# FFN up-projection of a diffusion trunk: seven block products per pair of output tiles

## Chip, cores and metric

The program runs on one core of a Trainium2 chip, in one launch. The metric is the device time of an execution in microseconds; the time of a kernel is the median of several executions. The engines are named as in the profile: PE is TensorE (matrix products), DVE VectorE, ACT ScalarE, POOL GpSimd, SP SyncE, which issues the transfers. A line number such as L101 is a line of the kernel's file.

## The reference

One inference step of a trunk of two layers on 512 latent and 128 context tokens of width 1024, in float32. Each layer has three mixers and then a gated MLP (FFN), which the change concerns. Cut to the FFN:

```python
def dwconv3(x, w, b):
    T = x.shape[1]
    xp = jnp.pad(x, ((0, 0), (1, 1), (0, 0)))
    return xp[:, :T] * w[0] + xp[:, 1:T + 1] * w[1] + xp[:, 2:] * w[2] + b
...
    u = dwconv3(h @ P['w_up'][l], P['ffn_conv_w'][l], P['ffn_conv_b'][l])
    x = x + g2 * ((jax.nn.silu(u[..., :D_FF]) * u[..., D_FF:]) @ P['w_down'][l])
```

Here h is the normed and modulated input (1024 features), D_FF is 2816, and w_up has 2 x 2816 columns: the first half is gated by SiLU and multiplied with the second. Latent and context tokens take the same weights; the convolution runs within each of the two groups.

## The kernel before

Tensors lie feature-major: a tile holds 128 features on the partitions and all 640 tokens (512 latent, 128 context) in its columns. The tokens are worked in two halves of 320 columns, one PSUM bank each. Every float32 product is made of two float32r parts: a value is cast to its high part `hi`, and `lo` is the value less `hi`; a product is hi·x_hi + hi·x_lo + lo·x_hi. So an output tile of the up-projection takes 8 feature tiles x 3 terms x 2 halves = 48 matmuls of 320 columns.

`weights` (L90) loads a chunk of weights (128 x 1024, 512 KB) into one of three slots "raw", and splits it 512 columns at a time: the cast on ACT (L100), the subtraction (L101) on POOL and DVE in turns (`alt`). The high and low parts have four slots each, "whi" and "wlo". `mm` (L117) issues the matmuls of an output tile, and `split` (L104) does the same split for an activation (L110 cast, L111 subtraction).

`ffn` (L908) works on 22 pairs of hidden tiles, a gate tile and a value tile each. `up(f)` makes the two products of pair f; `conv` follows each: ACT reads the product from PSUM and writes bias + w1·u to SBUF (L163), and four DVE operations add the left and the right neighbour (L165, L167), each for the 512 latent and for the 128 context columns, with the shifted operand read from PSUM. `glu` applies SiLU on ACT (L915), multiplies gate and value on POOL (L916), and splits the result for the down-projection. After a part of the pairs (FFN_PARTS, three parts of 7, 7 and 8) the down-projection adds that part to the residual x, in 8 output tiles.

The FFN's first pair is made within `handoff` (L449): the residual product before the FFN, the norm that follows it, and the first two up-products overlap, one half of the tokens after the other. The normed tiles are written there by DVE (L371 scales by the inverse root, L356 makes the low part) and ACT. `mod_step` makes the modulation vectors of what comes next: 2 MB of w_mod are loaded (L259) into eight slots "mw" of 256 KB and go through PE (L264). In the FFN it runs after pairs 2 and 4 and after every second down tile, while anything is left to do (7 vectors of 512 columns in layer 0, 2 in layer 1).

A scheduler orders the instructions of all engines when the program is built; only the matmuls that are pinned keep the order in which they were written. Each engine and each queue then works through its own list in order.

Of the kernel before, what the change touches and what calls it, by code (L numbers as in the profile page):

```python
# [16 lines left out]
P = 128  # L17
D = 1024
KD = D // P
NS = 512  # L20
# [36 lines left out]
class Tags:  # L57
    """A pool with a number of slots for each tag."""
# [8 lines left out]
class Trunk:  # L67
# [17 lines left out]
    def alt(self):  # L85
        """VectorE and GpSimd in turns, for work that either can do."""
# [3 lines left out]
    def weights(self, src, n):  # L90
        """Loads a chunk and splits it exactly into two float32r parts, 512 columns at a time."""
# [25 lines left out]
    def mm(self, acc, w, k0, xs, halves=(0, 1), ks=None, pin=False):  # L117
        """acc[m, t] = sum_k w[k, m] x[k, t]; w holds the tiles k0.. of len(xs)."""
# [41 lines left out]

    def conv(self, dst, acc, w0, w1, w2, bias):
# [8 lines left out]
    # ---------------------------------------------------------------- set-up  # L170
    def consts(self):
# [8 lines left out]
        # silu of the two conditionings, padded to 32 columns  # L180
# [23 lines left out]
    def layer_consts(self, l):  # L204
        nc, I = self.nc, self.I
        lp = self.lp
# [9 lines left out]
        # tensors of the mixers  # L216
        self.sgw = self.t(lp, [P, H, P], F32, "lc", 4)
        nc.sync.dma_start(self.sgw, I["sg_wT"][l])
        self.sgb = self.t(lp, [P, H, P], F32, "lc", 4)
# [688 lines left out]
    def ffn(self, l, h, accs, x, p2, nxt):  # L908
# [27 lines left out]
        for f0, f1 in FFN_PARTS:  # L936
            # the next part's first tile fills the time in which this part's last one is finished
            for f in range(len(acts), min(f1 + 1, NF)):
                up(f)
                if f in (2, 4):  # L940
                    self.mod_step((p2, "mw", 1))
# [200 lines left out]
```

## Time and profile before

| | |
|---|---|
| time, median of three runs | 2443.1 us (2442.36 to 2447.7) |
| span of the profiled execution | 2439.1 us |
| around the span, by the median | 4.0 us |
| PE busy | 2408.0 us, 99% |
| DVE busy | 1134.0 us, 46% |
| ACT busy | 944.8 us, 39% |
| POOL busy | 669.9 us, 27% |
| largest group of matmuls (L129, h by the high parts) | 6464 matmuls, 1246.9 us |

The span is the profiled execution from its first to its last instruction; the time of a run also holds what lies around it. Busy time counts an engine's own instructions, so two engines that are both busy may be in each other's way without the table showing it; that is to be read from the timelines.

### The profile page before, as it was taken

How to read it: one execution, taken by the hardware profiler on the slowest of the kernel's cores; microseconds unless marked ns; L12 is line 12 of the kernel's file. 1: busy time of each engine (PE TensorE's matmuls, PEld its weight loads, DVE VectorE, ACT ScalarE, POOL GpSimd, SP SyncE). 2: the span in 40 equal slices, each digit the busy share in tenths (PEclk: the TensorE clock that was granted, in tenths of full speed). 3: DMA queues.
4: the chain of work that ended last, by engine and by line, in shares of the span. 5: the costliest groups of instructions: out<-in, count | busy, mean ns of one | idle time of the engine just before them, and what ended most of it. 6: DMA issues, size and time to landing. Idle time of an engine off the chain costs nothing.

```text
span 2439.1 us, 40662 instructions
## 1 busy us (share of the span) xinstructions
PE 2408.0 (99%) x16708; PEld 2313.9 (95%) x16708; DVE 1134.0 (46%) x2111; ACT 944.8 (39%) x1728; POOL 669.9 (27%) x486
## 2 busy tenths in 40 slices
PE   8999999999999999999999999999999999999998
PEld 7999999999598999999999999999986989999998
DVE  5455545553146433424446455455532454244344
ACT  4433335544145322323454332455442543232334
POOL 2322232332222322313213222323322223232231
PEclk9999999999999999999999999999999999999999
DMA  8221221123544234222322212211233432222222
GB/s 282 74 73 64 65 78 62 60 72 132 173 147 160 69 109 140 72 75 79 103 80 70 74 64 66 76 54 62 97 114 120 147 96 74 79 74 73 81 72 69
DMA packets 88761, 227.39 MB, mean 93 GB/s; under 512 B 9472, under 2 KB 23936, under 8 KB 88576
## 3 DMA queue, kind: packets, MB, share of 16 engines
q1 hardware_dynamic: 88576, 224.80, 28.2%
q8 instruction: 131, 2.15, 0.4%
q14 instruction: 54, 0.44, 0.1%
HBM read 217.41 MB, written 7.35 MB: 92 GB/s over the span
## 4 chain that ended last, share of the span: by engine, by line
PE 96%; DVE 3%; ACT 1%; DMA 0%; issue 0%; SPq 0%; DVEq 0%; POOL 0%; POOLq 0%; ACTq 0%
PE acc L129 77%; PE acc L156 6%; PE ms L264 3%; PE ms L869 2%; PE ms L840 2%; PE ms L156 1%; PE ms L862 1%; PE ms L716 1%; PE ms L718 1%; PE ms L705 1%; DVE x L439 0%; PE ms L670 0%; PE ms L536 0%; PE ms L277 0%; PE ms L327 0%
## 5 line engine op out<-in xcount | busy, mean ns | idle before, releaser
L129 PE MATMUL acc<-h,whi 128*128 128x320 f32 x6464 | 1246.9, 311 | 5.0 <-DVE h L356 3.3
L129 PEld LDWEIGHTS acc<-h,whi 128*128 128x128 f32 x6464 | 1019.3, 188 | 32.1 <-issue 19.3
L100 ACT CAST whi<-raw 128x512 fp32r<-128x512 f32 x596 | 365.3, 614 | 1038.1 <-PE acc L129 787.9
L101 POOL TENSOR_TENSOR wlo<-raw,whi 128x512 fp32r<-128x512 f32 (+1 forms) x298 | 390.7, 1311 | 1355.1 <-ACT whi L100 1304.7
L129 PE MATMUL acc<-h,wlo 128*128 128x320 f32 x3232 | 755.4, 310 | 0.0
L129 PEld LDWEIGHTS acc<-h,wlo 128*128 128x128 f32 x3232 | 544.2, 188 | 3.5 <-issue 3.4
L101 DVE TENSOR_TENSOR wlo<-raw,whi 128x512 fp32r<-128x512 f32 (+1 forms) x298 | 241.2, 810 | 451.0 <-ACT whi L100 435.0
L129 PE MATMUL acc<-act,whi 128*128 128x320 f32 x1408 | 269.6, 310 | 0.0
L129 PEld LDWEIGHTS acc<-act,whi 128*128 128x128 f32 x1408 | 222.0, 188 | 4.2 <-issue 2.5
L129 PE MATMUL acc<-act,wlo 128*128 128x320 f32 x704 | 165.5, 309 | 0.0
L129 PE MATMUL acc<-y,whi 128*128 128x320 f32 x768 | 154.3, 314 | 1.7 <-DVE y L114 1.7
L499 DVE SCALAR_TENSOR_TENSOR x<-acc,mod,x 128x128 f32<-128x128 f32 (+3 forms) x136 | 66.3, 527 | 181.3 <-PE acc L129 181.3
L165 DVE SCALAR_TENSOR_TENSOR cw<-acc,vec,cw 128x511 f32<-128x511 f32 (+1 forms) x176 | 95.7, 544 | 115.1 <-ACT cw L163 114.0
L156 PE MATMUL acc<-whi,h 128*128 128x256 f32 x768 | 145.7, 283 | 0.0
L129 PEld LDWEIGHTS acc<-y,whi 128*128 128x128 f32 x768 | 121.2, 188 | 17.3 <-issue 11.7
L156 PEld LDWEIGHTS acc<-whi,h 128*128 128x128 f32 x768 | 123.0, 192 | 0.0
L129 PEld LDWEIGHTS acc<-act,wlo 128*128 128x128 f32 x704 | 119.1, 188 | 0.0
L916 POOL TENSOR_TENSOR cw<-cw,cw 128x640 f32<-128x640 f32 x44 | 69.2, 1573 | 156.5 <-DVE cw L167 151.9
L156 PE MATMUL acc<-wlo,h 128*128 128x256 f32 x384 | 108.7, 283 | 0.0
L167 DVE SCALAR_TENSOR_TENSOR cw<-acc,vec,cw 128x511 f32<-128x511 f32 (+1 forms) x176 | 96.7, 550 | 6.0
L129 PE MATMUL acc<-y,wlo 128*128 128x320 f32 x384 | 92.1, 315 | 0.0
L848 ACT ACTIVATE wk<-ms,mx 128x640 f32<-128x640 f32 (+1 forms) x80 | 56.7, 709 | 76.6 <-DVE mx L846 73.2
(257 smaller groups left out, 2425.0 us busy)
## 6 DMA issues: line engine op xcount, KB each, us to landing
raw<-w_in_f SPq DMA_DIRECT2D x98, 512.0 KB, 3.4
raw<-w_up SPq DMA_DIRECT2D x88, 512.0 KB, 3.3
wk<-w_mod SPq DMA_DIRECT2D x72, 256.0 KB, 3.4
mw<-w_mod SPq DMA_DIRECT2D x72, 256.0 KB, 5.7
raw<-w_down SPq DMA_DIRECT2D x32, 448.0 KB, 3.3
raw<-w_in_v SPq DMA_DIRECT2D x24, 512.0 KB, 3.7
raw<-w_branch SPq DMA_DIRECT2D x24, 512.0 KB, 3.3
mw<-w_mod SPq DMA_DIRECT2D x16, 512.0 KB, 8.8
```

The lines of the kernel that those rows point to most:

```text
L100: nc.scalar.copy(hi, raw[:, a:b])
L101: self.alt().tensor_sub(lo, raw[:, a:b], hi.bitcast(F32))
L129: ins = nc.tensor.matmul(acc[:, s], a[:, sl], b[:, s], start=k == 0 and i == 0, stop=k == last and i == 2)
L156: nc.tensor.matmul(accs[b], a[:, bs], w[:, sl], start=first and b % 2 == 0, stop=last and (b % 2 == 1 or b == NB - 1))
L165: nc.vector.scalar_tensor_tensor(dst[:, a + 1 : b], acc[:, a : b - 1], w0, dst[:, a + 1 : b], ALU.mult, ALU.add)
L167: nc.vector.scalar_tensor_tensor(dst[:, a : b - 1], acc[:, a + 1 : b], w2, dst[:, a : b - 1], ALU.mult, ALU.add)
L264: ins = nc.tensor.matmul(ps[j : j + 32, 0:width], self.cs[:, k, :], raws[k], start=k < 4, stop=k >= 4, tile_position=(0, j))
L499: self.nc.vector.scalar_tensor_tensor(x[:, a:b], acc[:, a:b], g[:, k, i : i + 1], x[:, a:b], ALU.mult, ALU.add)
L840: nc.tensor.matmul(ps[:, s : s + 320], st[:, qs], kk[:, s : s + 320], start=i == 0, stop=i == 1)
L848: nc.scalar.activation(e[:, 0:nk], ps[:, 0:nk], AF.Exp, bias=mx, scale=scale, accum_out=sm[:, j : j + 1])
L869: nc.tensor.matmul(po, at[:, c * P : (c + 1) * P], vv, start=c == 0, stop=c == n - 1)
L916: nc.gpsimd.tensor_mul(cs[0], cs[0], cs[1])
```

## The change

Pairs 2 to 21 of each layer, 20 of 22, are made by seven block products. The weights of a pair form a 2 x 2 block matrix: gate and value tile (rows), first and second four feature tiles (columns); the input h forms another: first and second four feature tiles (rows), first and second half of the tokens (columns). The eight block products of before become seven products of sums of blocks (`quarter`, 4 feature tiles x 3 terms = 12 matmuls of 320 columns each): 84 matmuls a pair in place of 96. The sums of weight blocks s1, s2, s3 are made on DVE and POOL and split again into high and low parts (`halves`: ACT cast, low part on the given engine). The sums of input blocks are made once per layer (`token_factors`), from the tiles `u` before the norm's shift is added; 16 additions on POOL, and subtractions, casts and low parts on DVE and ACT. Products that several outputs share stay in PSUM and are added to there; ACT and DVE copy and add the partial sums into two SBUF tiles, from which `conv` now reads. A pair's last two products (`seven_back`), its convolution and its `glu` come after the first two products of the next pair (`flush`).

Other edits: four parts of 5, 6, 5 and 6 pairs; `mod_step` in the FFN loads through the slots "raw" of the weights, four loads of 512 KB instead of eight of 256 KB; fewer slots for activations (14 instead of 20), more for convolution tiles (10 instead of 8), 24 new ones "tx" and three "ws"; layer constants lie in another pool.

The diff's core (in `up7` and `flush` `b` are the input factors):

```diff
-FFN_PARTS = ((0, 7), (7, 14), (14, 22))
+FFN_PARTS = ((0, 5), (5, 11), (11, 16), (16, 22))
...
+    def quarter(self, acc, w, xs, first, last):
+        nc = self.nc
+        hi, lo = w
+        for k, (xh, xl) in enumerate(xs):
+            sl = slice(k * P, (k + 1) * P)
+            for i, (a, b) in enumerate(((hi, xh), (hi, xl), (lo, xh))):
+                ins = nc.tensor.matmul(acc, a[:, sl], b, start=first and k == 0 and i == 0, stop=k == 3 and i == 2,
+                                       skip_group_check=not first)
+                self.tc.keep_in_program_order(ins)
+
+    def halves(self, src, eng):
+        hi = self.t(self.wp, [P, 512], F32R, "whi")
+        lo = self.t(self.wp, [P, 512], F32R, "wlo")
+        self.nc.scalar.copy(hi, src)
+        eng.tensor_sub(lo, src, hi.bitcast(F32))
+        return hi, lo
+
+    def seven_open(self, p, srcs):
+        nc = self.nc
+        r0, r1 = (self.t(self.wp, [P, 1024], F32, "raw") for _ in srcs)
+        for r, src in zip((r0, r1), srcs):
+            nc.sync.dma_start(r, src)
+        st = {"p": p, "r": ((r0[:, 0:512], r0[:, 512:]), (r1[:, 0:512], r1[:, 512:]))}
+        st["xy"] = self.t(self.ps, [P, 1024], F32, "acc", 2)
+        st["x"], st["y"] = st["xy"][:, 0:NHALF], st["xy"][:, 512 : 512 + NHALF]
+        st["c"] = [self.t(p, [P, NT], F32, "cw") for _ in range(2)]
+        return st
+
+    def seven_front(self, st, b):
+        nc, p = self.nc, st["p"]
+        (a11, a12), (a21, a22) = st["r"]
+        w1 = self.halves(a11, nc.vector)
+        w2 = self.halves(a12, nc.gpsimd)
+        s1, s2, s3 = (self.t(p, [P, 512], F32, "ws") for _ in range(3))
+        nc.vector.tensor_add(s1, a21, a22)
+        nc.gpsimd.tensor_add(s2, s1, a11)
+        nc.vector.tensor_add(s3, a11, a21)
+        st["s"] = s1, s2, s3
+        self.quarter(st["x"], w1, b["11"], True, False)
+        nc.scalar.copy(st["c"][0][:, 0:NHALF], st["x"])
+        self.quarter(st["y"], w2, b["21"], True, True)
+        nc.vector.tensor_add(st["c"][0][:, 0:NHALF], st["y"], st["c"][0][:, 0:NHALF])
+
+    def seven_mid(self, st, b):
...
+        w6 = self.halves(s2, nc.gpsimd)
+        w5 = self.halves(s1, nc.vector)
+        w7 = self.halves(s3, nc.gpsimd)
+        nc.gpsimd.tensor_add(s2, s2, a12)
+        self.quarter(x, w6, b["t2"], False, False)
+        nc.scalar.copy(c0[:, NHALF:NT], x)
+        self.quarter(z, w5, b["t1"], True, False)
+        self.quarter(x, w7, b["t3"], False, False)
+        nc.scalar.copy(c1[:, NHALF:NT], x)
+        nc.vector.scalar_tensor_tensor(c1[:, NHALF:NT], z, -1.0, c1[:, NHALF:NT], ALU.mult, ALU.subtract)
+
+    def seven_back(self, st, b):
...
+        w4 = self.halves(st["r"][1][1], nc.vector)
+        w3 = self.halves(st["s"][1], nc.gpsimd)
+        self.quarter(st["x"], w4, b["t4"], False, True)
+        nc.scalar.mul(c1[:, 0:NHALF], st["x"], -1.0)
+        self.quarter(st["z"], w3, b["22"], False, True)
+        nc.vector.tensor_add(c0[:, NHALF:NT], st["z"], c0[:, NHALF:NT])
+        return c0, c1
+
+    def token_factors(self, p, h, u, sh):
...
+        for k in range(4):
+            for kk in (k, k + 4):
+                for c, d, g in ((0, NS, 0), (NS, NT, 1)):
+                    nc.gpsimd.tensor_scalar_add(u[kk][:, c:d], u[kk][:, c:d], sh[:, kk, g : g + 1])
+            u0, u1 = u[k], u[k + 4]
+            f = self.t(p, [P, 2, NHALF], F32, "cw")
+            nc.vector.tensor_sub(f[:, 0], u0[:, half[0]], u0[:, half[1]])
+            nc.vector.scalar_tensor_tensor(f[:, 1], f[:, 0], -1.0, u1[:, half[1]], ALU.mult, ALU.subtract)
+            for j, n in enumerate(("t1", "t2")):
+                hi, lo = (self.t(p, [P, NHALF], F32R, "tx") for _ in range(2))
+                nc.scalar.copy(hi, f[:, j])
+                nc.vector.tensor_sub(lo, f[:, j], hi.bitcast(F32))
+                b[n].append((hi, lo))
...
+        def flush():
+            for f, st in pending:
+                glu([conv(2 * f + i, c) for i, c in enumerate(self.seven_back(st, b))])
+            pending.clear()
+
+        def up7(f):
+            st = self.seven_open(p2, [self.I["w_up"][l, i] for i in (2 * f, 2 * f + 1)])
+            self.seven_front(st, b)
+            flush()
+            self.seven_mid(st, b)
+            pending.append((f, st))
...
-                    self.mod_step((p2, "mw", 1))
+                    self.mod_step((self.wp, "raw", 2))
```

How the instructions now stand. First POOL, in the pairs of layer 0's second part. The names: raw, whi and wlo are weights and their parts, ws a sum of weight blocks, cw a convolution tile, act an activation's part. Before, two pairs of output tiles:

```order
L916 TENSOR_TENSOR cw_1315_8212<-cw_1315_8212,cw_1322_8277 128x640
L101 TENSOR_TENSOR wlo_1356_8466<-raw_1352_8459,whi_1355_8465 128x512
L101 TENSOR_TENSOR wlo_1363_8531<-raw_1359_8524,whi_1362_8530 128x512
L916 TENSOR_TENSOR cw_1331_8348<-cw_1331_8348,cw_1338_8413 128x640
L101 TENSOR_TENSOR wlo_1370_8598<-raw_1368_8595,whi_1369_8597 128x512
L111 TENSOR_TENSOR act_1340_8422<-cw_1331_8348,act_1339_8421 128x640
L101 TENSOR_TENSOR wlo_1377_8663<-raw_1375_8660,whi_1376_8662 128x512
```
And after, one pair (L202 makes s2, L220 adds a12 to it, L177 makes low parts, L1035 is the gated product):

```order
L202 TENSOR_TENSOR ws_1615_9752<-ws_1614_9751,raw_1605_9736 128x512
L177 TENSOR_TENSOR wlo_1613_9748<-raw_1605_9736,whi_1612_9747 128x512
L177 TENSOR_TENSOR wlo_1620_9788<-ws_1588_9600,whi_1619_9787 128x512
L1035 TENSOR_TENSOR cw_1594_9665<-cw_1594_9665,cw_1595_9671 128x640
L177 TENSOR_TENSOR wlo_1627_9837<-ws_1615_9752,whi_1626_9836 128x512
L111 TENSOR_TENSOR act_1597_9680<-cw_1594_9665,act_1596_9679 128x640
L220 TENSOR_TENSOR ws_1615_9752<-ws_1615_9752,raw_1605_9736 128x512
L177 TENSOR_TENSOR wlo_1631_9845<-ws_1616_9753,whi_1630_9844 128x512
```
Where POOL had two low parts of weights, a gated product and every other time a low part of an activation in a pair, it has four low parts and two sums beside the same two.

Second DVE, in the same pairs: before, one tile's convolution out of PSUM (acc) between low parts:

```order
L101 TENSOR_TENSOR wlo_1540_9852<-raw_1538_9849,whi_1539_9851 128x512
L111 TENSOR_TENSOR act_1520_9709<-cw_1511_9635,act_1519_9708 128x640
L165 SCALAR_TENSOR_TENSOR cw_1527_9771<-acc_1521_9712,vec0_7_90,cw_1527_9771 128x511
L167 SCALAR_TENSOR_TENSOR cw_1527_9771<-acc_1521_9712,vec0_7_90,cw_1527_9771 128x511
L165 SCALAR_TENSOR_TENSOR cw_1527_9771<-acc_1521_9712,vec0_7_90,cw_1527_9771 128x127
L167 SCALAR_TENSOR_TENSOR cw_1527_9771<-acc_1521_9712,vec0_7_90,cw_1527_9771 128x127
L101 TENSOR_TENSOR wlo_1547_9917<-raw_1545_9914,whi_1546_9916 128x512
```
And after, from the convolution of a pair to the last partial sum of the next one (L284 and L286 are the convolution, L177 low parts, L203 s3, L208 and L226 partial sums out of PSUM, acc and ms):

```order
L284 SCALAR_TENSOR_TENSOR cw_1594_9665<-cw_1554_9437,vec0_7_90,cw_1594_9665 128x511
L284 SCALAR_TENSOR_TENSOR cw_1594_9665<-cw_1554_9437,vec0_7_90,cw_1594_9665 128x127
L284 SCALAR_TENSOR_TENSOR cw_1595_9671<-cw_1555_9438,vec0_7_90,cw_1595_9671 128x511
L284 SCALAR_TENSOR_TENSOR cw_1595_9671<-cw_1555_9438,vec0_7_90,cw_1595_9671 128x127
L286 SCALAR_TENSOR_TENSOR cw_1594_9665<-cw_1554_9437,vec0_7_90,cw_1594_9665 128x511
L286 SCALAR_TENSOR_TENSOR cw_1594_9665<-cw_1554_9437,vec0_7_90,cw_1594_9665 128x127
L286 SCALAR_TENSOR_TENSOR cw_1595_9671<-cw_1555_9438,vec0_7_90,cw_1595_9671 128x511
L177 TENSOR_TENSOR wlo_1618_9784<-raw_1579_9585,whi_1617_9783 128x512
L286 SCALAR_TENSOR_TENSOR cw_1595_9671<-cw_1555_9438,vec0_7_90,cw_1595_9671 128x127
L226 SCALAR_TENSOR_TENSOR cw_1582_9590<-ms_1598_9683,cw_1582_9590 128x320
L203 TENSOR_TENSOR ws_1616_9753<-raw_1605_9736,raw_1606_9737 128x512
L208 TENSOR_TENSOR cw_1608_9741<-acc_1607_9740,cw_1608_9741 128x320
```
The convolution's shifted operand is now a cw tile in SBUF, both tiles' rows come in one piece, and low parts and partial sums stand between and behind them.

Third SP's queue, at the first pairs of layer 0's FFN. Before:

```order
L94 DMA raw_1290_8049<-w_up 128x1024
L259 DMA mw_1434_9120<-w_mod 128x512
L259 DMA mw_1435_9122<-w_mod 128x512
L94 DMA raw_1310_8154<-w_up 128x1024
L259 DMA mw_1436_9124<-w_mod 128x512
L259 DMA mw_1437_9126<-w_mod 128x512
L259 DMA mw_1438_9128<-w_mod 128x512
L259 DMA mw_1439_9130<-w_mod 128x512
L259 DMA mw_1440_9132<-w_mod 128x512
L94 DMA raw_1317_8219<-w_up 128x1024
```
And after:

```order
L94 DMA raw_1302_7997<-w_up 128x1024
L188 DMA raw_1310_8075<-w_up 128x1024
L188 DMA raw_1311_8076<-w_up 128x1024
L378 DMA raw_1330_8176<-w_mod 128x1024
L378 DMA raw_1331_8178<-w_mod 128x1024
L378 DMA raw_1332_8180<-w_mod 128x1024
L378 DMA raw_1333_8182<-w_mod 128x1024
L188 DMA raw_1336_8201<-w_up 128x1024
L188 DMA raw_1337_8202<-w_up 128x1024
L188 DMA raw_1363_8353<-w_up 128x1024
```
The loads of w_mod went to slots mw between those of the weights; now four of them take slots raw in the weights' own turn, and the loads of the next pair stand behind them.

## Rows read from the trace of the kernel before

**Rows 1.** Page, busy time by engine, and granted clock in 40 slices.
```profile
PE 2408.0 (99%) x16708; PEld 2313.9 (95%) x16708; DVE 1134.0 (46%) x2111; ACT 944.8 (39%) x1728; POOL 669.9 (27%) x486
...
PEclk9999999999999999999999999999999999999999
```

**Rows 2.** Page, chain that ended last: share of the span by engine.
```profile
PE 96%; DVE 3%; ACT 1%; DMA 0%; issue 0%; SPq 0%; DVEq 0%; POOL 0%; POOLq 0%; ACTq 0%
```

**Rows 3.** Windows: start:end, length, busy us (instructions) by engine, clock, DMA share, GB/s.
```profile
1060.00:1160.00 100.00, 100.00 (x684) 100.00 (x683) 41.27 (x66) 33.51 (x51) 28.84 (x22) 1.00 0.24 79
```

**Rows 4.** Timeline of ACT: start, duration, what; idle before in brackets.
```profile
771.32 0.88 ACT L163 ACTIVATE cw<-acc,vec 128x640 f32<-128x640 f32 x1
...
815.89 0.88 ACT L163 ACTIVATE cw<-acc,vec 128x640 f32<-128x640 f32 x1
...
822.93 0.88 ACT L163 ACTIVATE cw<-acc,vec 128x640 f32<-128x640 f32 x1
```

**Rows 5.** Timeline of PE in the norm that precedes the FFN.
```profile
742.43 0.31 PE L129 MATMUL acc<-h,wlo 128*128 128x320 f32 x1
...
742.87 0.31 PE L129 MATMUL acc<-h,wlo 128*128 128x320 f32 x1
```

**Rows 6.** Timeline of POOL, 800 to 823 us.
```profile
801.98 1.30 POOL L101 TENSOR_TENSOR wlo<-raw,whi 128x512 fp32r<-128x512 f32 x1 [5.74 <-ACT whi L100]
...
807.84 1.57 POOL L111 TENSOR_TENSOR act<-cw,act 128x640 fp32r<-128x640 f32 x1
...
819.13 1.58 POOL L916 TENSOR_TENSOR cw<-cw,cw 128x640 f32<-128x640 f32 x1 [5.29 <-DVE cw L167]
```

**Rows 7.** Timeline of DVE, 800 to 823 us.
```profile
802.72 0.75 DVE L165 SCALAR_TENSOR_TENSOR cw<-acc,vec,cw 128x511 f32<-128x511 f32 x1 [3.57 <-ACT cw L163]
...
809.03 0.93 DVE L101 TENSOR_TENSOR wlo<-raw,whi 128x512 fp32r<-128x512 f32 x1 [4.13 <-ACT whi L100]
...
811.32 0.34 DVE L165 SCALAR_TENSOR_TENSOR cw<-acc,vec,cw 128x127 f32<-128x127 f32 x1
...
816.07 0.69 DVE L101 TENSOR_TENSOR wlo<-raw,whi 128x512 fp32r<-128x512 f32 x1 [4.02 <-ACT whi L100]
...
819.58 1.67 DVE L101 TENSOR_TENSOR wlo<-raw,whi 128x512 fp32r<-128x512 f32 x1 [0.60 <-ACT whi L100]
```

**Rows 8.** Timeline of DVE, 348.5 to 351.5 us.
```profile
348.92 0.69 DVE L788 TENSOR_TENSOR qk<-qk,lc 128x512 f32<-128x512 f32 x1
```

**Rows 9.** Timeline of POOL, 348.5 to 351.5 us.
```profile
348.96 1.81 POOL L787 TENSOR_TENSOR wk<-wk,lc 128x512 f32<-128x512 f32 x1 [3.62 <-DVE wk L786]
```

**Rows 10.** Timelines of POOL and DVE, 144 to 147 us.
```profile
144.56 1.30 POOL L101 TENSOR_TENSOR wlo<-raw,whi 128x512 fp32r<-128x512 f32 x1 [5.74 <-ACT whi L100]
145.16 1.39 DVE L572 SCALAR_TENSOR_TENSOR qk<-wk,qk 128x640 f32<-128x640 f32 x1 [1.24 <-ACT wk L571]
```

**Rows 11.** Groups by shape, DVE and ACT: count, busy us, mean ns, idle before.
```profile
L309 DVE TENSOR_TENSOR sqa<-sqa,sq 128x320 f32<-128x320 f32 x56 | 27.4, 489 | 15.1 <-ACT sq L304 15.1
...
L100 ACT CAST whi<-raw 128x512 fp32r<-128x512 f32 x564 | 348.9, 620 | 983.3 <-PE acc L129 733.1 <-issue 179.0 <-PE ms L156 61.1
...
L915 ACT ACTIVATE cw<-cw 128x640 f32<-128x640 f32 x44 | 32.3, 735 | 0.0
L110 ACT CAST act<-cw 128x640 fp32r<-128x640 f32 x44 | 32.0, 728 | 52.3 <-POOL cw L916 52.3
```

**Rows 12.** Timeline of DVE at the end of the norm.
```profile
761.63 1.27 DVE L356 SCALAR_TENSOR_TENSOR h<-cw,mod,h 128x192 fp32r<-128x192 f32 x4
```

**Rows 13.** One line, L915: its table loads, ns min/median/max.
```profile
L915 ACT ACT_TABLE_LOAD  x2: 1283/1283/1283, 772.2 to 1975.2; - x2
```

**Rows 14.** Page, DMA issues: count, KB each, median us to landing.
```profile
raw<-w_up SPq DMA_DIRECT2D x88, 512.0 KB, 3.3
```

**Rows 15.** Tile mw: what its readers waited for, us and times.
```profile
  DMA mw<-w_mod: 4.7, 7
```

**Rows 16.** Windows near the start of the span.
```profile
8.00:20.00 12.00, 8.07 (x59) 7.54 (x61) 5.14 (x7) 6.37 (x11) 0.00 (x0) 0.86 1.05 390
```

More of the change, by code (lines that the diff above doesn't have):

```diff
@@ new lines, in seven_mid @@
+    def seven_mid(self, st, b):
+        nc, p = self.nc, st["p"]
+        (a11, a12), (a21, a22) = st["r"]
+        s1, s2, s3 = st["s"]
+        c0, c1 = st["c"]
+        x = st["x"]
+        z = st["z"] = self.psM()[:, 0:NHALF]
+        w6 = self.halves(s2, nc.gpsimd)
[8 more added lines that the diff above has]
+        nc.vector.scalar_tensor_tensor(c1[:, NHALF:NT], z, -1.0, c1[:, NHALF:NT], ALU.mult, ALU.subtract)
@@ new lines, in seven_back, with finish @@
+    def seven_back(self, st, b):
+        nc = self.nc
+        c0, c1 = st["c"]
+        w4 = self.halves(st["r"][1][1], nc.vector)
[6 more added lines that the diff above has]
+    def token_factors(self, p, h, u, sh):
+        nc = self.nc
+        half = (slice(0, NHALF), slice(NHALF, NT))
+        b = {n: [] for n in ("11", "21", "22", "t1", "t2", "t3", "t4")}
+        for k in range(4):
+            for n, kk, t in (("11", k, 0), ("21", k + 4, 0), ("22", k + 4, 1)):
+                b[n].append(tuple(x[:, half[t]] for x in h[kk]))
+        todo = []
+        for k in range(4):
+            for kk in (k, k + 4):
[10 more added lines that the diff above has]
+                b[n].append((hi, lo))
+            nc.vector.tensor_sub(u0[:, half[0]], u1[:, half[1]], u0[:, half[1]])
+            nc.vector.scalar_tensor_tensor(u1[:, half[0]], f[:, 1], -1.0, u1[:, half[0]], ALU.mult, ALU.subtract)
+            hi, lo = (self.t(p, [P, NHALF], F32R, "tx") for _ in range(2))
+            nc.scalar.copy(hi, u1[:, half[0]])
+            nc.vector.tensor_sub(lo, u1[:, half[0]], hi.bitcast(F32))
+            b["t4"].append((hi, lo))
+            todo.append((k, u0))
+        def finish():
+            for k, u0 in todo:
+                hi, lo = (x[:, half[1]] for x in h[k])
+                nc.scalar.copy(hi, u0[:, half[0]])
+                nc.vector.tensor_sub(lo, u0[:, half[0]], hi.bitcast(F32))
+                b["t3"].append((hi, lo))
+        return b, finish
@@ L205, in layer_consts @@
         nc, I = self.nc, self.I
-        lp = self.lp
+        lp, p1 = self.lp, self.p1
         self.vec = self.vecs[l]
@@ L222, in layer_consts @@
         for i in range(2):
-            self.rope.append(self.t(lp, [P, NS], F32, "lc", 4))
+            self.rope.append(self.t(p1, [P, NS], F32, "lc"))
             nc.sync.dma_start(self.rope[i], I["rope"][:, i, :])
-        self.ck = self.t(lp, [P, H, P], F32, "lc", 4)
+        self.ck = self.t(p1, [P, H, P], F32, "lc")
         nc.sync.dma_start(self.ck, I["cache_kT"][l])
-        self.cv = self.t(lp, [P, H, P], F32, "lc", 4)
+        self.cv = self.t(p1, [P, H, P], F32, "lc")
         nc.sync.dma_start(self.cv, I["cache_v"][l])
-        self.cn = self.t(lp, [P, 8, 129], F32, "cn", 1)
+        self.cn = self.t(p1, [P, 8, 129], F32, "cn")
         nc.sync.dma_start(self.cn, I["state"][l])
@@ L905, in branch, with ffn @@
         return out
-    def ffn(self, l, h, accs, x, p2, nxt):
+    def ffn(self, l, h, u, accs, x, p2, nxt):
         nc = self.nc
@@ L932, in up @@
             glu(cs)
+        pending = []
+        def flush():
[8 more added lines that the diff above has]
+            pending.append((f, st))
+        b, finish = self.token_factors(p2, h, u, self.mods[l, 3])
         glu([conv(i, acc) for i, acc in enumerate(accs)])
+        up(1)
+        finish()
+        done = 2
         st = self.norm_open(l + 1, 0 if nxt else None, p2, "cw")
         for f0, f1 in FFN_PARTS:
-            for f in range(len(acts), min(f1 + 1, NF)):
-                up(f)
+            for f in range(done, min(f1 + 1, NF)):
+                up7(f)
                 if f in (2, 4):
-                    self.mod_step((p2, "mw", 1))
+                    self.mod_step((self.wp, "raw", 2))
+                done = f + 1
+            end = f1 == NF
+            if end:
+                flush()
             g2 = self.mods[l, 5]
             down = lambda m: self.I["w_down"][l, m, :, f0 * P : f1 * P]
-            end = f1 == NF
             for m in range(KD - 2 if end else KD):
@@ L948, in ffn @@
                 self.mm(acc, w, 0, acts[f0:f1])
+                if m == 0:
+                    flush()
                 self.residual(x[m], acc, g2, m)
@@ L953, in ffn @@
                 elif m % 2:
-                    self.mod_step((p2, "mw", 1))
+                    self.mod_step((self.wp, "raw", 2))
         return self.handoff([down(m) for m in (KD - 2, KD - 1)], acts[f0:f1], x, g2, st,
```

13 lines of the change are left out of this document (7 added, 6 removed).

## The prediction

> **What bounds the kernel now.** I read the page's busy times and its clock row first, and the reader sees one engine: PE is busy in 99% of the span and its granted clock is at the full level throughout [rows 1]. The chain that ended last is 96% PE, 3% DVE, 1% ACT [rows 2]. Then one stretch of pure up-projection, 1060 to 1160 us, because the change lies there: PE 100.00 of 100 us, DVE 41.27, ACT 33.51, POOL 28.84 [rows 3]. So every matmul taken out is worth its pitch as long as the others keep up, and the question is how far DVE and POOL are from becoming the bound. The pitch comes from two evictions of successive tiles, 815.89 and 822.93 [rows 4]: 7.04 us for 48 matmuls, 146.7 ns each, 14.08 us for a pair of output tiles. Half products of 320 columns into one bank, which the change issues, have the same pitch already: 742.43 to 742.87 is three of them, 0.44 us [rows 5].
>
> Then I read how DVE and POOL run beside each other, row by row, since the change gives both more work. POOL's subtraction of 512 columns takes 1.30 us; a DVE operation that reads PSUM inside it, at 802.72, keeps its 0.75 us [rows 6, 7]. A DVE operation with both inputs in SBUF doesn't: alone at 816.07 it takes 0.69, but at 809.03, while POOL's 807.84 (1.57) runs to 809.41, it takes 0.93 and ends at 809.96, 0.55 after POOL; at 819.58, behind POOL's product that ends at 820.71, it takes 1.67 and ends 0.54 after it [rows 6, 7]. The other way it is the same: DVE's 348.92 ends at 349.61 and POOL's operation, begun at 348.96, at 350.77, 1.16 later [rows 8, 9]. It holds for the three-operand form too: begun at 145.16 with POOL busy until 145.86, it ends at 146.55, 0.69 later for 640 columns [rows 10]. So the two exclude each other for 0.55 of a DVE operation's 0.69, and for 1.16 of a POOL operation's 1.30; only the starts overlap.
>
> **The change, part by part.**
> *Products removed.* Seven products of 12 matmuls, 84, stand for 96: 84 x 146.7 ns = 12.32 us a pair. 40 pairs (20 in each layer): 480 matmuls, -70.4 us if PE stays the bound.
>
> *DVE and POOL in a pair.* POOL gets six 512-column operations in a pair (s2, four low parts, the sum with a12), the gated product (640), and half of the activations' low parts (640 every other pair). DVE gets three low parts, s1, s3, half a low part of 640, and the convolution: before, it read PSUM; now four operations of 511 and four of 127 columns have both inputs in SBUF. In excluded time: POOL 6 x 1.16 + 1.44 + 0.72 = 9.12 (1.58 - 0.14 for 640); DVE (5 + 4) x 0.55 + 4 x 0.20 + 0.5 x 0.69 = 6.1 (0.20 is the 0.34 of [rows 7] less the same 0.14). Sum **15.2 us**, more than the 12.32 that PE would need and more than the 14.08 of before. Before, a pair had two low parts on each engine, the gated product and the activation's low part: 2 x 1.16 + 2 x 0.55 + 1.44 + 1.0, 5.9 of 14.08. So I expect these two to set the pace. Lower bound of a pair's period T: 15.2. Upper bound: no overlap even of the starts, POOL 6 x 1.30 + 1.58 + 0.79 = 10.15 and DVE 9 x 0.69 + 4 x 0.34 + 0.4 = 8.0, 18.1. I take **16.0**, nearer the lower: the rows show the overlap each time, and 0.8 is for the turns at which neither has its input, since each engine's queue is in order and every low part waits for a cast of 0.62 [rows 11].
> The Trainium skill, page "SBUF — State Buffer", section "Who interferes with whom", calls the pair of ports that DVE and GpSimd share an exclusive lock, held for the whole instruction, the other one fully blocked; this speaks against the change. The rows agree on the blocking, but not on the whole instruction: by the page's rule the period would be 18.1, by the rows 15.2.
>
> *What that makes of a layer.* Four stretches of 4, 6, 5 and 5 pairs; the first of each starts with rested engines and some operands ready, so I let one in each run at 12.32, the other 16 at T: 4 x 12.32 + 16 x 16.0 = 305.3 against 20 x 14.08 = 281.6, +23.7. Both layers **+47** (T = 15.2: +22; 18.1: +115; 12.32: -70).
>
> *Token factors.* They run between the norm and the first product of seven. POOL's 16 additions (8 of 512, 8 of 128 columns, priced as its two-input rows: 8 x (1.30 + 0.46) = 14.1 us) fall into the norm's second half, where DVE's operations have both inputs in SBUF; I take 5.5 us of delay there, since each DVE operation that meets one waits about half of it. The norm ends at 762.90 in the trace [rows 12], then at 768.4. Behind that DVE has some 26 factor operations of 0.49 [rows 11], the first two tiles' convolution (4.4), and the sums and low parts of the first pair (2.75): 19.9 us, to 788.3; POOL's turns between them, some ten of 1.16, 11.6: to 799.9; w2's low part on POOL 1.3 later. PE would be there at 785: the second handed-on tile is through at 770.9 (its eviction at 771.32 [rows 4]) and pair 1 takes 14.08. So 4.6 us a layer if POOL's turns are hidden, 16.2 if they are not, 27.9 if also the 16 casts on ACT (0.73 each at most) stand in the row. ACT's own work there, a table load of 1.28, a SiLU of 0.74 and a cast of 0.73 [rows 11, 13], lies beside it. I take 16, because the operations alternate: **+32** (10 to 55).
>
> *Modulation loads.* They had eight buffers of their own; now each of nine steps puts four loads of 512 KB on SP's queue through the three slots that the FFN's weights use, and the weights' loads of the next tile stand behind them. A slot is free only when the cast and the subtraction, or PE's modulation products, have read it, and the second raw tile of a pair is read last by the back products a pair later. A landing takes 3.3 us [rows 14]. Before, PE's whole idle time on these loads was 4.7 us, 7 times [rows 15]. A step costs what the weights come late: 3.3 + 0.62 for a cast + a low part, less what is loaded ahead. I take 3.5 for f = 2 and 2 for f = 4 in each layer (the pair's period is long, some hides), 4.4 for each of the three steps between down tiles 3, 5 and 7 (short tiles), 1.5 each for two others: **+27** (8 if only one load of two is exposed; 55 if two loads follow one another in each).
>
> *The rest.* Layer constants loaded later and the last part's flush ahead of its first down product: **+4** (0 to 8). The four extra down products' starts (four parts instead of three) have the same matmuls in sum.
>
> Sum: 47 + 32 + 27 + 4 = **+110**. The profiled span is 2439.1, with 4.0 us around it to the median 2443.1: 2439.1 + 110.4 + 4.0 = **2554 us**. All terms at their lower bounds: 2483.
>
> **Rivals.**
> *Other side: the shared pair doesn't decide, PE stays the bound (10%).* The single mechanism is T = 12.32: POOL's and DVE's turns fit into each other and the buffers absorb them. For it: DVE and POOL were busy less than 42 and 29% [rows 3]. Against it: 15.2 of excluded time. Then -70.4; the token factors, without turns, 10 a layer, 20; loads 27; rest 4: -20, **2423**. It decides from T = 12.55 down with my other terms, 13.96 with their lower bounds (32 T - 464.6 + the others = 0).
> *The excluded time is the whole instruction, or the queues couple so that the engines alternate (14%).* T = 18.1: +115 + 63, **2621**. For it: a low part of DVE waits for a cast and a sum of POOL's and the reverse, so one late operation delays both queues. Against: the overlaps of [rows 6 to 10].
> *The clock falls when PE waits (6%).* The one stretch with a granted clock below full is 8 to 20 us, 0.86, with PE busy 8.07 of 12 [rows 16]. At T = 16.0 PE is busy 77%. If a third of the pairs (13) ran at the lower level, 24.64 instead of 16: +112, **2666**; more pairs, more. Against: the page has 9s in every other slice.
> *Neither gain nor loss (3%)*: T near 13.
>
> **How the numbers follow.** The forecast, T from 15.2 to 16.8 with the other terms within their bounds, has 67%; its own range is 2490 to 2600. Other side 10%, whole instruction 14%, clock 6%, no change 3%. Slower 67 + 14 + 6 = 87%. A change under 0.2% (5 us) can't be told from none here. The range for 8 in 10 leaves out the other side and most of the clock's cases: 2460 (just below all lower bounds, 2483) to 2640 (just above the whole instruction's case).
>
> **What would show it.** Right: in a stretch of pairs PE's busy share near 77%, waiting for low parts (L177) of DVE and POOL; DVE's convolution rows of 511 columns lengthened by POOL's operations (up to 1.8 us instead of 0.75); pairs 15 to 17 us apart; idle PE for modulation loads inside f = 2, f = 4 and the first down phase; the first L168 product some 16 us late in each layer. Wrong: PE near 100% in the pairs with 12.3 us between them. The prediction would be most wrong if the convolution and the low parts fell into gaps where POOL waits anyway.

## The result, and the profile after

The changed kernel takes 2626.65 us (median of four runs, 2623.52 to 2631.05), the kernel before 2444.24 on the same chip: ratio 1.0746, interval 1.0731 to 1.0761, 182 us slower. The forecast was 2554 and 111 slower; the time lies within the range, near the 2621 of the whole-instruction case, which is not what happened. The profiled execution spans 2629.0 us. Of the page, the rows that answer to [rows 1]:

```profile
PE 2427.2 (92%) x16228; PEld 2298.5 (87%) x16228; DVE 1412.6 (54%) x2463; ACT 1088.0 (41%) x2072; POOL 975.5 (37%) x694
...
PEclk9999999999989989999899999999999898999999
```

PE has 480 matmuls fewer and is busy longer. 2408.0 - 70.4 would be 2337.6; it is 2427.2, 89.6 more. Most of that is the clock (mean granted clock of the span 0.966, before 0.998): some 485 matmuls start at the lower of its two levels and take some 0.12 us longer each, about 60 us by an estimate from the trace. The rest is largely that a matmul which a wait follows is counted with its whole 0.31 us and not with its pitch, and that there are more waits. It is idle for 201.8 us instead of 31.1, 170.7 more. -70.4 + 89.6 + 170.7 = 189.9, the difference of the spans. What PE waits for (us in all, times, longest):

```profile
PE acc L168 <- ACT cw L206: 75.0, 40, 4.2
PE acc L129 <- DVE cw L286: 29.0, 2, 15.2
PE ms L383 <- DMA raw<-w_mod: 19.7, 14, 3.4
```

The first is in every one of the 40 pairs, and it is one that the prediction did not name: a product waits for ACT's copy of a partial sum. The other two are the token factors and the modulation loads. Four undisturbed pairs of layer 0's second stretch, from one SiLU to the fourth after it (columns as in [rows 3]):

```profile
983.42:1047.43 64.01, 53.82 (x330) 52.77 (x329) 52.98 (x66) 34.01 (x60) 45.19 (x29) 0.92 0.19 62
```

A pair takes 64.01 / 4 = 16.0 us, what was forecast. 4 x 84 matmuls at the pitch of before would be 49.3; PE is busy for 53.82 of it (4.5 more, for the lower clock, 1.1 a pair) and idle for 10.2 (2.5 a pair). How a pair's wait comes about is seen in three timelines, at the longest of the four waits. ACT:

```profile
1016.41 0.74 ACT L1034 ACTIVATE cw<-cw 128x640 f32<-128x640 f32 x1 [4.63 <-DVE cw L286]
...
1018.40 0.42 ACT L206 COPY cw<-acc 128x320 f32<-128x320 f32 x1
```

DVE:

```profile
1011.39 4.00 DVE L284 SCALAR_TENSOR_TENSOR cw<-cw,vec,cw 128x511 f32<-128x511 f32 x4
1015.32 1.66 DVE L286 SCALAR_TENSOR_TENSOR cw<-cw,vec,cw 128x511 f32<-128x511 f32 x3
```

PE:

```profile
1014.19 0.46 PE L168 MATMUL acc<-h,whi 128*128 128x320 f32 x2
1014.48 0.31 PE L168 MATMUL acc<-h,wlo 128*128 128x320 f32 x1
1018.88 0.80 PE L168 MATMUL acc<-h,whi 128*128 128x320 f32 x2 [4.08 <-ACT cw L206]
1019.47 0.47 PE L168 MATMUL acc<-h,wlo 128*128 128x320 f32 x1
```

The first product of the new pair ends at 1014.8. Its copy (L206) stands in ACT's queue behind the previous pair's SiLU (L1034), which waits 4.63 us for that pair's convolution (L284, L286). PE's second product, which writes the other bank of the same PSUM tile, begins 0.06 us after the copy's end, after 4.08 us, and runs at half the pace at first: 0.59 us from its first to its third matmul, where it was 0.29 just before the wait. The convolution is late because DVE's rows are longer than the operations: the groups by shape, of the whole span,

```profile
L284 DVE SCALAR_TENSOR_TENSOR cw<-cw,vec,cw 128x511 f32<-128x511 f32 x80 | 82.2, 1027 | 11.8 <-ACT cw L282 11.8
L177 DVE TENSOR_TENSOR wlo<-raw,whi 128x512 fp32r<-128x512 f32 x80 | 74.0, 926 | 24.6 <-ACT whi L176 23.9
L286 DVE SCALAR_TENSOR_TENSOR cw<-cw,vec,cw 128x511 f32<-128x511 f32 x80 | 72.0, 900 | 0.0
L203 DVE TENSOR_TENSOR ws<-raw,raw 128x512 f32<-128x512 f32 x40 | 62.9, 1573 | 24.8 <-POOL wlo L177 24.8
```

have means of 900 to 1573 ns, where a low part takes 690 with POOL idle and the convolution out of PSUM 750 [rows 7]. So two causes are mixed: the ports that DVE and POOL share, and the order of the copy. The experiments take them apart.

### The profile page after: what moved, and what is told of

It is laid out like the page before. It is cut to its first block, busy times and chain, and to the rows that moved or that the text cites. A ratio compares the mean times of both kernels' runs of the same rounds, so it can differ in the third digit from the quotient of the medians.

```text
span 2629.0 us, 40870 instructions
## 1 busy us (share of the span) xinstructions
PE 2427.2 (92%) x16228; PEld 2298.5 (87%) x16228; DVE 1412.6 (54%) x2463; ACT 1088.0 (41%) x2072; POOL 975.5 (37%) x694
## 3 DMA queue, kind: packets, MB, share of 16 engines
q1 hardware_dynamic: 85696, 224.80, 26.3%
## 5 line engine op out<-in xcount | busy, mean ns | idle before, releaser
L129 PE MATMUL acc<-h,whi 128*128 128x320 f32 x3904 | 777.1, 314 | 40.7 <-DVE cw L286 29.0
L101 POOL TENSOR_TENSOR wlo<-raw,whi 128x512 fp32r<-128x512 f32 (+1 forms) x234 | 304.4, 1302 | 1022.8 <-ACT whi L100 1008.8
L129 PEld LDWEIGHTS acc<-h,whi 128*128 128x128 f32 x3904 | 626.2, 190 | 62.3 <-ACT tx L265 29.5
L129 PE MATMUL acc<-h,wlo 128*128 128x320 f32 x1952 | 468.7, 313 | 0.0
L129 PEld LDWEIGHTS acc<-h,wlo 128*128 128x128 f32 x1952 | 334.8, 190 | 3.5 <-issue 3.4
L168 PE MATMUL acc<-h,whi 128*128 128x320 f32 x960 | 235.8, 335 | 88.0 <-ACT cw L206 75.0
L101 DVE TENSOR_TENSOR wlo<-raw,whi 128x512 fp32r<-128x512 f32 (+2 forms) x234 | 167.8, 717 | 207.1 <-ACT whi L100 191.1
L168 PEld LDWEIGHTS acc<-h,whi 128*128 128x128 f32 x960 | 171.9, 203 | 105.9 <-ACT cw L206 86.2
L177 POOL TENSOR_TENSOR wlo<-ws,whi 128x512 fp32r<-128x512 f32 x120 | 172.2, 1437 | 105.8 <-ACT whi L176 104.9
L168 PE MATMUL acc<-h,wlo 128*128 128x320 f32 x480 | 158.8, 331 | 2.8 <-DVE wlo L177 2.8
L176 ACT CAST whi<-ws 128x512 fp32r<-128x512 f32 x160 | 98.4, 617 | 150.6 <-PE acc L168 80.6
L168 PE MATMUL acc<-tx,whi 128*128 128x320 f32 x640 | 151.8, 325 | 6.5 <-DVE cw L208 6.5
L284 DVE SCALAR_TENSOR_TENSOR cw<-cw,vec,cw 128x511 f32<-128x511 f32 (+1 forms) x160 | 118.3, 781 | 11.8 <-ACT cw L282 11.8
```

The costliest lines, as they stand in the source:

```text
L101: self.alt().tensor_sub(lo, raw[:, a:b], hi.bitcast(F32))
L129: ins = nc.tensor.matmul(acc[:, s], a[:, sl], b[:, s], start=k == 0 and i == 0, stop=k == last and i == 2)
L168: ins = nc.tensor.matmul(acc, a[:, sl], b, start=first and k == 0 and i == 0, stop=k == 3 and i == 2, skip_group_check=not first)
L176: self.nc.scalar.copy(hi, src)
L177: eng.tensor_sub(lo, src, hi.bitcast(F32))
L284: nc.vector.scalar_tensor_tensor(dst[:, a + 1 : b], acc[:, a : b - 1], w0, dst[:, a + 1 : b], ALU.mult, ALU.add)
```

## The experiments

Differences are to the kernel before on the same chip; the changed kernel has +182.4. "Period" is that of the same four pairs. In e3, e4, e8 and e12 work is left out or other values are computed, so that they show what something costs and could not replace the kernel.

**e1, the copy behind the second product.**

```diff
-        nc.scalar.copy(st["c"][0][:, 0:NHALF], st["x"])
         self.quarter(st["y"], w2, b["21"], True, True)
+        nc.scalar.copy(st["c"][0][:, 0:NHALF], st["x"])
```

> One edit to the changed kernel: ACT's copy of the first product (L206) is written behind the second product w2 instead of ahead of it; nothing else. Theory A (the order written, not the port pair, holds PE: in all 40 pairs the first matmul of w2 waits for this copy, 75 us in sum, and the copy stands in ACT's queue behind a SiLU that waits for the convolution): the wait goes, and with it a good part of the matmuls at the lower clock behind it; 2629 falls by 75 to 120, to 2505 to 2550, and the pairs come 13 to 14.5 us apart instead of 16. Theory B (the step of the prediction: DVE and POOL exclude each other for 15.2 us a pair): PE only meets another wait, the period stays at 15.2 or above; 32 x 0.8 = 26 us at most, 2600 or more.

2602.73 us, ratio 1.0653 (1.0636 to 1.0671), +158.6: 24 us won, what theory B allowed. The wait for L206 is gone; it is now for L208, the sum that follows the copy:

```profile
PE acc L168 <- DVE cw L208: 50.6, 30, 2.8
```

The four pairs:

```profile
978.65:1039.58 60.93, 52.67 (x335) 50.38 (x334) 55.71 (x66) 33.48 (x60) 46.36 (x29) 0.97 0.22 68
```

60.93 / 4 = 15.23 us: the 15.2 of excluded time that the prediction worked out as the lower bound. The copy was worth the 0.8 above it, no more. That the ports have no time left here can be added up from the timelines of the two engines: in 60.88 of these 60.93 us an operation of POOL, or one of DVE with two inputs in SBUF, is under way. In the changed kernel it is 61.72 of 64.01, in e3 (below) 46.01 of 54.59. A stretch of e1 shows how they take turns. POOL:

```profile
997.31 1.57 POOL L1035 TENSOR_TENSOR cw<-cw,cw 128x640 f32<-128x640 f32 x1
998.84 1.74 POOL L177 TENSOR_TENSOR wlo<-ws,whi 128x512 fp32r<-128x512 f32 x1
1000.66 1.61 POOL L220 TENSOR_TENSOR ws<-ws,raw 128x512 f32<-128x512 f32 x1
```

DVE:

```profile
997.38 2.05 DVE L203 TENSOR_TENSOR ws<-raw,raw 128x512 f32<-128x512 f32 x1 [0.79 <-POOL wlo L177]
999.35 1.78 DVE L177 TENSOR_TENSOR wlo<-ws,whi 128x512 fp32r<-128x512 f32 x1
```

The ends are 998.88 (POOL), 999.43 (DVE), 1000.58 (POOL), 1001.13 (DVE) and 1002.27 (POOL): a DVE operation ends 0.55 us after POOL's, a POOL operation 1.14 to 1.15 after DVE's, the prices of [rows 6 to 10].

**e3, POOL's low parts left out; e12, the convolution's shifted operand from PSUM.** Two ways to take time off the ports, the second without taking an operation from either queue.

```diff
-        w2 = self.halves(a12, nc.gpsimd)
+        w2 = self.halves(a12, nc.gpsimd, False)      # so for w6, w7, w3: returns (hi, hi)
```

> The four low parts that POOL makes in a pair (of w2, w6, w7 and w3) are left out, and the matmuls read the high part in their place: as many matmuls, 4 x 40 POOL operations fewer, 4.64 us of the 15.2 us of excluded time in a pair gone. Theory B (the port pair sets the period): the period falls from 16 to some 12.5 to 13.5, -80 to -110 us, 2520 to 2550. Theory A (the copy behind the SiLU): the copy still waits for the convolution, which only runs a little sooner; -20 to -50 us, 2575 to 2605, and the waits for L206 remain, 40 to 60 us in sum.

```diff
+                    if b - a > 300:
+                        d = d.rearrange("p (r c) -> p r c", r=7)
+                        v = z[:, 0:73].unsqueeze(1).to_broadcast([P, 7, 73])
+                    else:
+                        v = z[:, 0 : b - a - 1]
+                    nc.vector.scalar_tensor_tensor(d, v, w, d, ALU.mult, ALU.add)
```

> The changed kernel, but the convolution of the pairs of seven products takes its shifted operand from PSUM (columns of the partial sum z, repeated) instead of from the SBUF tile; the same operations of 511 and 127 columns at the same places of DVE's queue, with other values. Excluded time of DVE and POOL in a pair falls from 15.2 to 12.2 us; neither queue has an operation less. Theory B (the port pair): the period falls by 1.5 to 2.5 us, 2540 to 2575, and DVE's rows of the convolution go back to 0.75 us. Theory C (the queues' order and length, whatever the ports): within 10 us, 2617 to 2637.

e3: 2552.89, ratio 1.0445 (1.043 to 1.0461), +108.8, 74 us won: just outside theory B's range and far below theory A's. PE's wait for the copy is still there in all 40 pairs, but shorter, 38.5 us in sum. Its four pairs:

```profile
977.34:1031.93 54.59, 50.83 (x342) 49.77 (x341) 43.67 (x66) 33.97 (x60) 20.76 (x14) 1.00 0.23 73
```

e12: 2603.9, ratio 1.0654 (1.0638 to 1.0671), +160.5, 22 won; the time lies between the two theories' ranges. Its four pairs, and the convolution's rows in them:

```profile
988.08:1045.05 56.97, 51.64 (x338) 50.59 (x337) 46.68 (x66) 34.25 (x60) 41.69 (x29) 0.97 0.22 70
```

```profile
L291 DVE SCALAR_TENSOR_TENSOR cw<-ms,vec,cw 128x511 f32<-128x511 f32 x17 | 12.6, 742 | 0.1
```

The periods are 13.65 (10.6 of excluded time) and 14.24 (12.2). In e12 no queue has an operation less; DVE's convolution went back to 742 ns and the period fell by 1.76, within what theory B said. So in these pairs it is the ports, and theory C, the order and number of operations alone, falls there. Both periods lie above their excluded time, by 3.05 and 2.04: with less on the ports, something else sets the pace, in part still the copy. The whole kernel of e12 won much less than 40 x 1.76, though; the pairs beside the modulation steps did not follow. In layer 0 the time from the SiLU of pair 1 to that of pair 6 grew from 181.3 to 188.3 us, as much as the four pairs behind it won. What held those pairs was not taken apart; e12 also keeps the partial sum z in PSUM until the convolution has read it, which no run separates.

**e8, e1 and e3 together.** The two edits above.

> The runs e1 and e3 together: the copy behind w2, and POOL's four low parts of a pair left out (the matmuls read the high part). If the ports' excluded time (10.6 us a pair) is now under PE's 12.32 and the copy's wait is gone, PE is the bound again in the pairs: periods of 12.3 to 13, 20 to 40 us below e3, 2513 to 2533. If the wait only moves on to the next partial sum: 10 us or less below e3, 2543 to 2553.

2530.52, ratio 1.0347 (1.0329 to 1.0366), +84.7, 24 less than e3, as much as the copy alone was worth. The four pairs:

```profile
967.04:1020.06 53.02, 49.97 (x335) 48.84 (x334) 43.17 (x66) 32.90 (x60) 23.26 (x14) 1.00 0.24 76
```

13.26 a pair, PE busy for 94%: near its 12.32, though a little above the 12.3 to 13 that were expected; the time lies in the range. Even so the kernel is 85 us slower than before, so the pairs are not all of the loss.

**e5, the four low parts on DVE.**

```diff
-        w6 = self.halves(s2, nc.gpsimd)
+        w6 = self.halves(s2, nc.vector)      # so for w2, w7, w3
```

> The same operations as the changed kernel, but the four low parts of a pair that POOL makes (of w2, w6, w7, w3) are made by DVE. Theory B (the port pair): each costs 0.55 us of excluded time on DVE instead of 1.16 on POOL, 15.2 falls to 12.8 a pair, the period from 16 to 13.5 to 14.5, 50 to 80 us less: 2547 to 2577. Theory C (not the ports, but each engine's queue in its order: the earlier run without POOL's low parts won 74 us because POOL had less to do): DVE gets 2.8 us a pair more, on top of its rows of some 13 us with waits, and becomes the slower queue: 2620 to 2660.

2594.33, ratio 1.0607 (1.0591 to 1.0623), +148.5, 34 won: between the two theories.

```profile
981.08:1042.01 60.93, 51.04 (x337) 49.20 (x336) 55.54 (x82) 34.03 (x60) 22.67 (x14) 1.00 0.20 66
```

The period is 15.23 at 12.8 of excluded time; DVE is busy for 91%. Moving work to DVE takes the ports' time down and brings DVE's own queue near its end; that this queue is the next bound is seen in e11 below, where it is busy for 99%.

**e6, e7 and e9, the change without its pairs.** e6 makes the pairs as before, with the factors; e7 also without factors; e9 also with slots of their own for the modulation.

```diff
-                up7(f)
+                up(f)                                # e6, e7, e9
-        b, finish = self.token_factors(p2, h, u, self.mods[l, 3])      # e7, e9
-        self.mod_step((self.wp, "raw", 2))
+        self.mod_step((p2, "mw", 1))                 # e9
```

> The changed kernel with its pairs made as before (eight block products, convolution out of PSUM), but with its four parts, the modulation loads through the weights' slots, and the token factors, which are made and not used (the last 8 operations of them, finish, are left out because they overwrite the input). The changed kernel less this one is what the pairs of seven products cost: by the prediction +47 us, so 2580 here; if the waits and the slow matmuls inside the pairs cost what PE's rows suggest (some 60 us a layer), 2500 to 2520. Less the next run it is what the factors cost: by the prediction 32 us, by PE's waits behind the convolution with the slow matmuls 40 to 60.

> As the run before, without the token factors: the kernel before with four parts and with the modulation loads through the weights' slots. By the prediction's terms +27 and +4: 2475. If the loads cost what leaving out three of four gave in the changed kernel (61 us): 2500 to 2510. If the ring of slots is only short when a pair holds two of them at once: within 10 us of before, 2454 or less.

> As e7 (plain pairs, four parts, no factors), but the FFN's modulation steps load into eight slots of their own, as before. Only the parts and the place of the layer's constants are left of the change: by the prediction's term +4, 2448 to 2452. If four parts or the constants are what made e7 66 us slower, and not the slots, 2490 or more.

e6 2546.12, ratio 1.0414 (1.0398 to 1.0429), +100.3; e7 2512.1, 1.0274 (1.0257 to 1.0291), +66.2; e9 2450.99, 1.0027 (1.0016 to 1.0038), +7.6. So the pairs cost 182.4 - 100.3 = 82, the factors 34, the loads 58.6, the rest 7.6. Of the expectations, e9's held; e7 came out 2 us above its middle case and far from the 2475 of the prediction's terms, and e6 between its two cases. From e7 to e9 the loads change in size as well (four of 512 KB, eight of 256 KB); the runs don't part the size from the slots.

What the loads do is seen in e7. SP's queue around the first pairs:

```profile
770.33 30.05 SPq L378 DMA_DIRECT2D raw<-w_mod  x4
800.47 10.26 SPq L94 DMA_DIRECT2D raw<-w_up  x4
813.59 26.64 SPq L378 DMA_DIRECT2D raw<-w_mod  x4
```

Four loads of w_mod take 30 us to get slots, and w_up's loads stand behind them. The SiLUs of pairs 2 and 3, with a modulation step between them, are 26.3 us apart in e7,

```profile
795.23 0.74 ACT L1034 ACTIVATE cw<-cw 128x640 f32<-128x640 f32 x1 [2.30 <-DVE cw L286]
821.55 0.74 ACT L1034 ACTIVATE cw<-cw 128x640 f32<-128x640 f32 x1
```

and 14.0 in e9:

```profile
799.63 0.73 ACT L1034 ACTIVATE cw<-cw 128x640 f32<-128x640 f32 x1
813.67 0.73 ACT L1034 ACTIVATE cw<-cw 128x640 f32<-128x640 f32 x1
```

Two stretches of e7, the norm's second half and the first pairs,

```profile
752.00:775.00 23.00, 20.78 (x125) 19.29 (x124) 15.41 (x41) 13.52 (x28) 3.92 (x4) 0.93 0.18 59
775.00:845.00 70.00, 62.52 (x384) 55.01 (x383) 24.20 (x43) 19.60 (x28) 18.65 (x13) 0.92 0.29 94
```

and of e9:

```profile
752.00:775.00 23.00, 22.99 (x145) 15.24 (x144) 16.86 (x45) 12.47 (x27) 2.58 (x2) 1.00 0.68 223
775.00:845.00 70.00, 70.00 (x479) 70.00 (x479) 30.16 (x50) 26.10 (x40) 25.42 (x18) 1.00 0.27 90
```

With slots of their own the modulation's products fill the norm's waits, at 223 GB/s of loads, and the pairs run without a gap. Through the weights' slots the loads move 59 GB/s there, the products come into the pairs, and the 70 us behind hold 384 matmuls instead of 479, at a clock of 0.92. Over the whole span PE, with as many matmuls, is idle for 67.1 us in e7 instead of 35.9, and busy for 2443.9 instead of 2413.0.

**e4, one modulation load of four.**

```diff
+            if tag == "raw" and k:
+                raws += raws[0:per]
+                continue
             r = self.t(pool, [P, per, width], F32, tag)
```

> In the FFN's nine modulation steps three of the four loads are left out, and the products read the first load four times: 27 loads fewer in the weights' ring, as many matmuls. By the prediction's term the loads cost 27 us in all: 2600. If the steps cost what PE's idle rows say (some 50 us on these loads, and slow matmuls behind them): 2560 to 2580. If the weights' loads behind them were hidden: no change within 5 us.

2565.66, ratio 1.0497 (1.0481 to 1.0513), +121.6, 61 won, within its second case and nearly the same sum as e7 less e9, found from the other end.

**e2 and e10, the factors later.** e2 writes them behind the first pair's convolution, e10 behind that of pair 1 too.

```diff
-        b, finish = self.token_factors(p2, h, u, self.mods[l, 3])
         glu([conv(i, acc) for i, acc in enumerate(accs)])
+        b, finish = self.token_factors(p2, h, u, self.mods[l, 3])      # e2
         up(1)
+        b, finish = self.token_factors(p2, h, u, self.mods[l, 3])      # e10
         finish()
```

> One edit to the changed kernel: the convolution and the gating of the first pair are written ahead of the token factors, not behind them. Theory A (pair 1's product waits, 15 us in each layer, for an accumulator that the convolution has to empty, and that convolution stands in DVE's queue among the factors): the two waits go, -25 to -40 us with the slow matmuls behind them, 2587 to 2602. Theory B (POOL's 16 additions hold DVE up by their turns on the ports, so that the factors themselves come late whatever stands first): the wait moves to the first product that needs a factor, less than 10 us are won, 2617 or more.

> The changed kernel with the token factors written behind the products, the convolution and the gating of pairs 0 and 1, not ahead of them. Theory A (a matter of order: the accumulators of pairs 0 and 1 are emptied late because the convolutions stand among the factors; 15 us of waiting in each layer): the factors run beside pair 1's product, -20 to -35, 2592 to 2607. Theory B (the factors take DVE and POOL longer than pair 1 and the first two products cover): the wait moves to the first product with a factor, 2612 to 2640, as e2 had it.

e2 2638.94, ratio 1.0798 (1.0782 to 1.0814), +194.8, 12 slower than the changed kernel; e10 2624.17, 1.0732 (1.0716 to 1.0748), +180.8, 1.6 less, which the intervals don't tell from none. In e2 PE's wait for the convolution is now at the first product of seven,

```profile
PE acc L168 <- DVE cw L286: 38.0, 2, 19.7
```

and in e10 in the wait for the copy, whose longest grew from 4.2 to 9.4:

```profile
PE acc L168 <- ACT cw L206: 93.1, 40, 9.4
```

Theory A fell, in both, and the order moves the wait. It does not move to a product with a factor, as the theories B had it: in layer 0 the products that wait (the first of the first pair of seven in e2, the second in e10) read h alone, and the copy that e10 waits for stands among the factors' casts on ACT. In e10 the wait is shorter than the 15.2 of the changed kernel and the second product of the first pair begins 10.6 us sooner, but by the SiLU of pair 6 only 1.2 us of that are left; where the rest goes was not taken apart.

**e11, the three edits that leave nothing out** (e1, e5, e10).

> The copy behind w2, the four low parts on DVE, and the factors behind pair 1, together: the changed kernel as good as these orders make it. If the effects add up: 2627 - 24 - 32 - 30 = 2541. If the copy and the low parts take away the same wait (the waits for the copy fell from 75 to 39 us with the low parts on DVE): 2555 to 2570. In no case below the kernel before, since the modulation's loads alone cost 60.

2559.94, ratio 1.0468 (1.0453 to 1.0484), +116.5: 66 us better than the changed kernel, in the range of the second case, but not for its reason: e1 and e5 add up (24 + 34) with a little more, and what is missing are the 30 expected of e10. It stays far from the kernel before. Its four pairs:

```profile
973.50:1030.05 56.55, 49.97 (x331) 48.30 (x330) 55.80 (x82) 32.67 (x60) 26.77 (x14) 1.00 0.22 71
```

14.14 a pair, no better than the plain pair's 14.08, with DVE busy for 99% of it. No version here beats the kernel before.

## Why the prediction was right, and where its sum was off

**The direction and its mechanism were right.** PE is no longer the bound in the pairs; DVE and POOL are. The period was forecast at 16.0 and is 16.0, and with the copy's order mended it is 15.23, the bound of 15.2 from [rows 6 to 10], with the ports in use in 60.88 of 60.93 us. e12 shows that it is the ports and not the number of operations. By the rule of the Trainium skill (page "SBUF — State Buffer", section "Who interferes with whom": the lock is held for the whole instruction) it would have been 18.1; e1's trace agrees with the blocking, but its rows put the price at 0.55 and some 1.15, as those of before did, and its period is that of the rows' sum. What the 0.8 above the bound stood for was wrong: not turns without an input, but one copy behind a SiLU on ACT, and PE waiting for it. As far as this 0.8 goes the 16.0 was hit by luck. Of the signs, PE's waits for low parts did not show: PE waits for the copy, and is busy for 84% (53.82 of 64.01), the lower clock included.

**The pairs' sum was too small: +47 forecast, +82 measured.** The step that failed is "the first of each [stretch] starts with rested engines ..., so I let one in each run at 12.32". All 40 pairs at 16.1 (the mean of fourteen undisturbed periods in four stretches) instead of 14.08 make 40 x 2.02 = 81, so nothing is left for eight pairs at PE's pace. At the border of two stretches it can be read: in layer 0 the SiLUs of pairs 10 and 12, with the down phase between, are 77.55 us apart in the changed kernel and 74.03 in e6, 3.5 more for two pairs; the four such borders have 3.3 to 4.1 more, 15.7 to 16.1 a pair, where one pair at 12.32 and one at 16.0 would make 0.16 more. For the pairs beside a modulation step the sum is worked out, not read: they have other waits as well.

**The loads were mis-sized: +27 forecast, +58.6 (e7, e9) and 61 (e4) measured.** The prediction priced how late weights would land, 3.5 and 2 us for the steps behind pairs 2 and 4. In e7 it is 26.3 and 27.1 us from SiLU to SiLU at those pairs of layer 0, and 14.0 at others. The first down phase, with three steps that were priced at 4.4 each, takes 24.0 us more than in e9 (82.4 and 58.4 from SiLU to SiLU). What was missed for the steps in the pairs is where their products stood before: in the norm's waits, where they cost some 4 us (e9's first SiLU begins at 774.80, e7's at 770.71), because slots of their own let the loads run ahead. The change took the loads out of the waits, and the products with them.

**Factors and the rest were right in size:** +32 forecast and 34 measured, +4 and 7.6. The way to the 32 was partly another one: PE waits 15.15 us in layer 0 (29.0 in both) for an accumulator of the first pairs, whose convolution stands among the factors, not for a low part. POOL's 16 additions take 20.9 us there where 14.1 were forecast. e2 and e10 show that a wait stays whatever stands first, up to 19.7 and 9.4 us, and that neither order wins time.

**The rivals.** The other side (PE stays the bound) fell: e8 comes near it in the pairs only with 4.64 us of POOL's work left out. The whole-instruction case gives 2621, near the measured time, but by a period of 18.1 that no undisturbed stretch has on average. The clock was kept as a case of its own, at 6%, and the main sum has no term for it; in truth it fell behind three of the four waits of this stretch. That is 1.1 us of the 16.0 in a pair, inside the period that was hit, and some 60 us of PE's busy time over the span. In e3, whose waits are 0.94 us each there, the clock is 1.00.

## What to carry to other kernels

Add up, for each pair of engines that share something, the time in which one excludes the other, and compare that sum with the bound of the stage: here both engines were under half busy before and their sum still became the pace. Before loads are moved to other buffers, look where the work that they feed stands now; work that fills a wait costs little only as long as its data come early. Saved matmuls are worth their pitch only if nothing that each of them needs is made by engines with less room than PE's saving.

## What the runs showed of the hardware

Behind three of the four waits in the four pairs (2.19, 4.08 and 2.40 us, not 1.51) the granted clock is at the lower of its two levels for a while, and matmuls start 0.267 us apart instead of 0.147; the stretch has 0.92 on average. It is not the sum of the waits that decides: in e5 PE is idle for as long (2.47 us a pair, the longest wait 2.31) and the clock is 1.00. What does decide is left open by these runs. DVE and POOL shut each other out so far that in e1 the ports they share are in use all the time and set the period, 15.23 us, though the two engines are busy for 91% and 76%. DVE's operations with one operand in PSUM keep 742 ns beside a POOL that is busy for 73% of the stretch (41.69 of 56.97).
